# One more five-product step and a rewritten program order in a fused 3x3 convolution with 2x2 max pooling

## The chip, the core and the metric

The kernel runs on one core of one Trainium2 chip. The metric is the device time of one execution in microseconds (us): the median of several runs. The core has five engines that run side by side and meet through semaphores. TensorE (PE) multiplies matrices into the eight banks of PSUM; PEld is its weight load, which overlaps its matmuls. VectorE (DVE) and ScalarE (ACT) work elementwise on SBUF and PSUM. GpSimd (POOL) works on SBUF alone and issues the casting loads of the input. SyncE (SP) issues the other loads and the stores. Each engine takes its instructions strictly in program order.

## The reference

```python
batch, c_in, h, w, c_out, k = 16, 64, 64, 64, 128, 3        # pool_size 2, float32
x_pad = np.pad(x, ((0, 0), (0, 0), (1, 1), (1, 1)))
conv[b, co] += weight[co, ci, kh, kw] * x_pad[b, ci, kh:kh+h, kw:kw+w]   # over ci, kh, kw
output[b, c, i, j] = np.max(conv[b, c, 2*i:2*i+2, 2*j:2*j+2])
```

The input is 16.8 MB, the output 8.4 MB, and every output pixel is the maximum over a 2x2 patch of the convolution.

## The kernel before

**Tiling.** Two images sit on the 128 partitions, 64 input channels each. So there are eight image pairs p, and each pair is cut into four quarters of 16 input rows, which give 8 pooled rows (8x64 elements, 512 on a partition, until the columns are pooled too). A quarter of a pair is a *step* s (0 to 31), and h (0 or 1) is the image within the pair. A *product* is three matmuls, one for each column of the 3x3 kernel, of 64 contraction rows, 128 output channels and 8x64 (or 8x63 at an edge) columns. The products of the two images run on the two halves of the array at the same time; the kernel keeps one lane of products for each half and issues them tap by tap in turn (function `product`, lines 269 to 275), so the k-th product of one lane always goes with the k-th of the other. In this text `P2.7.0|PA1.10.1` is such a couple: name, step, image.

**Two kinds of step.** With g0, g1, g2 the three rows of the kernel and x0, x1 the two input rows of a pooled pair (x before is x-1, x after is x2), the even and odd convolution rows are g0 x-1 + g1 x0 + g2 x1 and g0 x0 + g1 x1 + g2 x2. A *K step* takes **five products**: PA1 and PA2 make (g2-g1) x1 + g0 x-1 in bank ta, PB1 and PB2 make (g0-g1) x0 + g2 x2 in bank tb, and after their maximum PR adds g1 (x0+x1) for both. A *W step* takes **four**: P2 makes half of (g0+g2-g1)(x0-x1) in ta, a copy of it seeds tb, P0 and P3 add products of the row differences x1-x-1 and x2-x0, and after the maximum P1 adds half of (g0+g1+g2)(x0+x1). The string TYPES says which step is which: before, K are 0, 2, 4, 12 and 21 and 27 are W.

**What surrounds the products of one step and image**, in this order:

- row work on SBUF, for both images at once: a K step needs KS (row sum, DVE). A W step needs E (row difference, 512 elements a partition), D (edge differences, 1024) and S (row sum, 512), each on DVE or on POOL by the three lists at lines 40 to 42 (lines 88 and 89)
- SE, W steps alone: ACT copies ta into tb (line 389)
- EV: ACT copies ta out of PSUM, negated in a W step (373, 375)
- MX: DVE takes the row maximum of tb and EV's copy, in place in PSUM (399)
- PR or P1 on PE, and then OD: ACT copies the odd columns out (405)
- CM: DVE takes the column maximum into an output tile (419); ST: SP stores the tile (443)

Each image of a step holds one or two of the eight PSUM banks from its first product until CM. There are 11 output tiles, so the twelfth step to begin its CM waits until the first has been stored.

**The start.** Step 0, 1, 2 and 3 read image pair 0, which SP loads in float32 in pieces: `kfirst` (two pieces, for step 0), `ksecond` (two, for step 2), `middle` (three, for steps 1 and 3; the last piece is issued by the step L). The rows of the two K steps are cast into `kx0` by eight small casts: XOa and XOb (odd rows), XEa and XEb (even rows) of `kfirst`, X1a, X1b, X2a and X2b of `ksecond`. The weights land in `wraw`; g0, g1, g2 and their sums and differences D2, D0, GM, GP are cast into `wq`. For each of them PE transposes its columns (steps TD2, TG0 and so on: a *turn*) and ACT or DVE copies the result to `wt` (VD2, VG0 and so on, lines 180 to 188); TMP and VMP do GM and GP together. POOL repeats a column for three of them (uG1, uGM, uGP) and makes the sum GS. The products of steps 0 and 2 are cut in halves, F.k.part and H.k.part, those of step 1 in G.k.part, and the last P1 in Q.0 and Q.1. The other seven pairs come as 14 loads LX.p.part on POOL's queue, each a half of a pair, cast to bf16 on the way.

**What sets the order.** The schedule is written out: the string ORDER (line 494) lists every step above, and the loop at lines 555 to 557 issues each one's instructions to its engine as it comes. There is no reordering afterwards. A GpSimd operation on SBUF is put behind the last SBUF operation that was given to VectorE ahead of it in ORDER (`on_vector`, `on_gpsimd`, `behind`, lines 74 to 84), also where the data would not ask for it.

Of the kernel before, what the change touches and what calls it, by code (L numbers as in the profile page):

```python
# [11 lines left out]
def kernel(  # L12
# [435 lines left out]

    def cast_rows(n, src, to, lo, hi):
        out, in_ = kx0[:, to + lo : to + hi : 2, :], src[:, lo:hi:2, :]  # L450
        if n in CAST_BY_SCALAR:
            odd_cast[n] = nc.scalar.copy(out=out, in_=in_)
        else:
            odd_cast[n] = nc.vector.tensor_copy(out=out, in_=in_)  # L454

    steps = {
        "g0": lambda: nc.scalar.copy(out=slots(G0), in_=g0),
        "g1": lambda: nc.vector.tensor_copy(out=slots(G1), in_=g1),  # L458
        "g2": lambda: nc.scalar.copy(out=slots(G2), in_=g2),
# [133 lines left out]
```

## Time and profile before

| | |
|---|---|
| median of 3 runs | 102.99 us (102.98 to 103.02) |
| the profiled execution, its own time | 103.01 us |
| its span, first to last instruction | 101.1 us |
| PE busy (94.3 us) | 93% of the span |
| DVE busy (89.9 us) | 89% |
| ACT busy (86.0 us) | 85% |
| POOL busy (70.2 us) | 69% |
| read from HBM, written to it | 17.20 MB, 8.39 MB |

How to read it: a line of the profile names the source line, the engine, the operation, what it writes and reads, and how often it ran; behind the bar stand the busy time of the group, the mean duration of one, and the idle time of the engine just ahead of them with what ended it. Successive instructions of DVE, ACT and PE overlap by some tens of nanoseconds, so a duration is a little more than what an instruction costs its engine; that cost is read from runs of equal instructions in the timeline. The span is 1.9 us shorter than the execution's own time, and what lies around the span is taken as unchanged.

### The profile page before, as it was taken

How to read it: one execution, taken by the hardware profiler on the slowest of the kernel's cores; microseconds unless marked ns; L12 is line 12 of the kernel's file. 1: busy time of each engine (PE TensorE's matmuls, PEld its weight loads, DVE VectorE, ACT ScalarE, POOL GpSimd, SP SyncE). 2: the span in 40 equal slices, each digit the busy share in tenths (PEclk: the TensorE clock that was granted, in tenths of full speed). 3: DMA queues.
4: the chain of work that ended last, by engine and by line, in shares of the span. 5: the costliest groups of instructions: out<-in, count | busy, mean ns of one | idle time of the engine just before them, and what ended most of it. 6: DMA issues, size and time to landing. Idle time of an engine off the chain costs nothing.

```text
span 101.1 us, 2529 instructions
## 1 busy us (share of the span) xinstructions
PE 94.3 (93%) x903; PEld 58.9 (58%) x903; DVE 89.9 (89%) x190; ACT 86.0 (85%) x194; POOL 70.2 (69%) x79
## 2 busy tenths in 40 slices
PE   6889999999999999999999999999999999999900
PEld 2257878844555656777678677675555546545500
DVE  1589989999999999999999989999898969999950
ACT  5356778999699899999999999898999999999830
POOL 7268999906995985774987693994969699417000
PEclk9999999999999999999999999999999999999997
DMA  2999899999947999999947984835024837423062
GB/s 58 297 342 300 171 199 216 221 232 226 244 78 131 247 228 220 228 221 358 343 31 124 282 180 42 169 114 208 3 76 141 304 111 252 163 104 110 0 227 84
DMA packets 11900, 18.41 MB, mean 182 GB/s; under 512 B 880, under 2 KB 9200, under 8 KB 11888
## 3 DMA queue, kind: packets, MB, share of 16 engines
q0 software_dynamic: 2016, 7.34, 39.9%
q1 hardware_dynamic: 9728, 10.78, 32.0%
q8 instruction: 7, 0.11, 0.4%
q10 hardware_dynamic: 144, 0.13, 0.4%
q14 instruction: 5, 0.04, 0.1%
HBM read 17.20 MB, written 8.39 MB: 253 GB/s over the span
## 4 chain that ended last, share of the span: by engine, by line
PE 87%; DVE 4%; DMA 3%; ACT 1%; issue 1%; DVEq 0%; ACTq 0%
PE acc L207 86%; DMA wraw<-in_weight_dram 3%; DVE acc L399 1%; PE acc L165 1%; DVE wq L88 1%; DVE o L434 1%; DVE kx L454 1%; ACT acc L389 1%; ACT od L427 1%; DVE wq L458 0%; DVE wt L188 0%; DVEq L399 0%; ACTq L389 0%
## 5 line engine op out<-in xcount | busy, mean ns | idle before, releaser
L207 PEld LDWEIGHTS <-wt 64*128 64x128 bf16 x870 | 56.4, 94 | 32.6 <-issue 4.7
L207 PE MATMUL acc<-wd,wt 64*128 64x512 bf16 (+2 forms) x336 | 65.9, 369 | 0.1
L399 DVE TENSOR_TENSOR acc<-acc,ev 128x512 f32<-128x512 f32 x64 | 42.4, 692 | 1.4 <-ACT ev L375 0.5
L207 PE MATMUL acc<-we,wt 64*128 64x512 bf16 (+3 forms) x168 | 39.2, 369 | 0.0
L207 PE MATMUL acc<-ws,wt 64*128 64x512 bf16 (+3 forms) x168 | 37.7, 369 | 0.2 <-DVE acc L399 0.2
L375 ACT ACTIVATE ev<-acc 128x512 f32<-128x512 f32 x54 | 32.2, 607 | 1.4 <-PE acc L207 1.2
L389 ACT COPY acc<-acc 128x512 f32<-128x512 f32 x52 | 30.7, 596 | 0.9 <-DVE o L419 0.2
L419 DVE TENSOR_TENSOR o<-acc,od 128x256 f32<-128x256 f32 x62 | 24.4, 417 | 2.4 <-ACT od L405 1.5
L89 POOL TENSOR_TENSOR ws<-xb 128x512 bf16<-128x512 bf16 x15 | 17.1, 1148 | 11.6 <-DVE wd L88 7.3
L405 ACT COPY od<-acc 128x256 f32<-128x256 f32 x62 | 22.5, 382 | 2.1 <-PE acc L207 1.8
L89 POOL TENSOR_TENSOR we<-xb 128x512 bf16<-128x512 bf16 x16 | 18.4, 1150 | 6.0 <-PE acc L207 2.3
L89 POOL TENSOR_TENSOR wd<-xb 128x1024 bf16<-128x1024 bf16 x9 | 19.1, 2123 | 1.9 <-DVE we L88 1.1
L207 PE MATMUL acc<-xb,wt 64*128 64x504 bf16 (+3 forms) x72 | 15.0, 372 | 0.0
L88 DVE TENSOR_TENSOR wd<-xb 128x1024 bf16<-128x1024 bf16 x16 | 10.7, 682 | 0.0
L124 POOL DMA_DIRECT2D xb<-in_x_dram x14 | 7.9, 574 | 0.1
L207 PE MATMUL acc<-ks,wt 64*128 64x504 bf16 (+1 forms) x30 | 7.2, 377 | 0.0
L373 ACT COPY ev<-acc 128x512 f32<-128x512 f32 x10 | 5.6, 590 | 1.4 <-PE acc L207 1.3
L207 PE MATMUL acc<-kx,wt 64*128 64x252 bf16 (+3 forms) x96 | 6.0, 267 | 0.4 <-DVE kx L454 0.4
L89 POOL TENSOR_TENSOR wd<-middle 128x512 bf16<-128x512 f32 (+1 forms) x3 | 4.9, 1643 | 0.2 <-DVE we L88 0.2
L551 PE MATMUL acc<-const-bfloat16-1.0 128*128 128x512 bf16 x8 | 3.5, 621 | 0.8 <-PEq L574 0.8
L88 DVE TENSOR_TENSOR ws<-xb 128x512 bf16<-128x512 bf16 x10 | 4.1, 418 | 0.0
L88 DVE TENSOR_TENSOR we<-xb 128x512 bf16<-128x512 bf16 x9 | 3.7, 425 | 0.0
(33 smaller groups left out, 29.4 us busy)
## 6 DMA issues: line engine op xcount, KB each, us to landing
out_dram<-o SPq DMA_DIRECT2D x31, 256.0 KB, 2.9
xb<-in_x_dram POOLq DMA_DIRECT2D x7, 528.0 KB, 9.0
xb<-in_x_dram POOLq DMA_DIRECT2D x7, 496.0 KB, 11.0
middle<-in_x_dram SPq DMA_DIRECT2D x1, 512.0 KB, 5.3
ksecond<-in_x_dram SPq DMA_DIRECT2D x1, 320.0 KB, 5.8
middle<-in_x_dram SPq DMA_DIRECT2D x1, 320.0 KB, 6.2
wraw<-in_weight_dram SPq DMA_DIRECT2D x1, 288.0 KB, 2.9
kfirst<-in_x_dram SPq DMA_DIRECT2D x1, 288.0 KB, 3.2
```

Of the source, the lines that this page charges most:

```text
L88: return on_vector(nc.vector.tensor_tensor(**args))
L89: return on_gpsimd(nc.gpsimd.tensor_tensor(**args))
L124: inst = nc.gpsimd.dma_start(out=xb[p][:, 1 + lo : 1 + hi, :], in_=rows_of(p, lo, hi))
L165: nc.tensor.transpose(tp[:, k * CO : (k + 1) * CO], wq[:, j : j + 2, :].rearrange("a b c -> a (b c)"), ident,)
L207: nc.tensor.matmul(acc[t][:, i0:i1, o0:o1], wt[lo : lo + CI, tap_of(m0, kw, h), :], rows(lo, i0, i1, c0, c1), start=start and kw == 1, sto ...
L373: nc.scalar.copy(out=ev[s, h], in_=acc[t])
L375: nc.scalar.mul(ev[s, h], acc[t], -1.0)
L389: nc.scalar.copy(out=acc[tb[s, h]], in_=acc[ta[s, h]])
L399: nc.vector.tensor_tensor(out=t, in0=t, in1=ev[s, h], op=MAX)
L405: nc.scalar.copy(out=od[s, h], in_=acc[tb[s, h]][:, :, 1::2])
L419: nc.vector.tensor_tensor(out=ot[s][:, h], in0=acc[t][:, :, 0::2], in1=od[s, h], op=MAX)
L551: nc.tensor.matmul(acc[n].rearrange("p a b -> p (a b)"), ones[:, 0:128], ones, start=True, stop=True, skip_group_check=True)
```

## The change

- TYPES: K steps are 0, 2, 4, 10, 16 and 23, so 26 steps are W instead of 27.
- SUM_ON_GPSIMD, DIFF_ON_GPSIMD, EDGES_ON_VECTOR: the row work is split anew. In numbers, with steps 0 to 3 left out: S on POOL 17 (15 before), on DVE 7 (10); E on POOL 16 (16), on DVE 8 (9); D on DVE 16 (16), on POOL 8 (9); KS on DVE 4 (3).
- Casts and turns: XEa, XOb, XEb and X2a go to ACT (XOb alone before). VG2 goes from ACT to DVE. g0 and g2 stay on ACT, g1 on DVE, though they are now named in the list.
- g1 and the casts that run on DVE are now noted by `on_vector`, so that POOL's SBUF operations further on in ORDER are put behind them.
- ORDER is rewritten as a whole, with the loads LX and the stores ST at other places in it.

```diff
-    TYPES = "KWKWKWWWWWWWKWWWWWWWWKWWWWWWWWWW"
-    SUM_ON_GPSIMD = (5, 7, 8, 9, 10, 14, 15, 18, 19, 20, 23, 24, 28, 29, 30,)
-    DIFF_ON_GPSIMD = (5, 6, 8, 10, 15, 16, 17, 18, 19, 20, 22, 25, 27, 28, 29, 30,)
-    EDGES_ON_VECTOR = (7, 8, 9, 10, 11, 14, 15, 17, 18, 19, 23, 24, 27, 29, 30, 31,)
-    TURNED_BY_SCALAR = ("D2", "G1", "G2", "MP")
-    CAST_BY_SCALAR = ("XOb",)
+    TYPES = "KWKWKWWWWWKWWWWWKWWWWWWKWWWWWWWW"
+    SUM_ON_GPSIMD = (5, 6, 8, 9, 11, 12, 13, 18, 19, 20, 21, 22, 24, 25, 27, 28, 30,)
+    DIFF_ON_GPSIMD = (5, 7, 11, 12, 13, 14, 17, 18, 19, 24, 25, 26, 27, 28, 29, 31,)
+    EDGES_ON_VECTOR = (6, 8, 9, 11, 13, 14, 15, 17, 18, 19, 22, 24, 25, 26, 27, 31,)
+    TURNED_BY_SCALAR = ("D2", "G1", "MP")
+    CAST_BY_SCALAR = ("g0", "g2", "XEa", "XOb", "XEb", "X2a")
...
+    def tap_cast(n, m, src):
+        if n in CAST_BY_SCALAR:
+            nc.scalar.copy(out=slots(m), in_=src)
+        else:
+            on_vector(nc.vector.tensor_copy(out=slots(m), in_=src))
...
-            odd_cast[n] = nc.vector.tensor_copy(out=out, in_=in_)
+            odd_cast[n] = on_vector(nc.vector.tensor_copy(out=out, in_=in_))
...
     ORDER = """
-        D0 g2 g0 TD0 g1 D2 TD2 VD0 XEa uG1 TG1 F.2.0 TG0 XOa L VD2 F.0.0 TG2 GS GP uGP VG1 XOb F.0.1 LX.1.0 VG2
-        VG0 F.1.0 F.1.1 XEb F.2.1 EV.0.1 EV.0.0 GM uGM LX.2.0 F.3.1 F.3.0 TMP VMP KS.0 X1a X2a X1b X2b KS.2
-        H.0.0 H.1.0 H.0.1 H.1.1 EV.2.1 EV.2.0 Ea LX.1.1 LX.3.0 Da MX.0.0 MX.0.1 H.2.0 PR.0.1 H.3.0 G.0.0 Eb
-        G.0.1 H.2.1 H.3.1 PR.0.0 SEa.0 SEa.1 SEb.0 SEb.1 E.3 P2.3.1 G.1.0 S.1 MX.2.0 OD.0.0 CM.0.0 G.2.0 OD.0.1
-        CM.0.1 ST.0 LX.3.1 LX.2.1 Db G.1.1 EV.1.1 MX.2.1 G.2.1 MX.1.1 PR.2.0 PA1.4.0 PA2.4.0 EV.1.0 MX.1.0
...
-        P1.29.1 OD.30.0 CM.30.0 EV.31.1 MX.31.1 EV.31.0 MX.31.0 Q.0 Q.1 OD.30.1 CM.30.1 ST.30 OD.29.0 CM.29.0
-        OD.29.1 CM.29.1 ST.29 ODh.0.0 CMh.0.0 ODh.0.1 CMh.0.1 ODh.1.0 CMh.1.0 ODh.1.1 ST.31.0 CMh.1.1 ST.31.1
+        g0 g2 D0 TD0 D2 TD2 TG0 TG2 XEa g1 uG1 VD2 XOb XEb X2a XOa L VG0 VD0 F.0.0 F.1.0 F.2.0 F.2.1 GS GM TG1
+        F.0.1 F.1.1 LX.1.0 GP VG2 F.3.1 F.3.0 uGM KS.0 X1a H.0.0 H.1.0 LX.1.1 LX.2.0 uGP TMP X1b H.0.1 H.1.1 X2b
+        KS.2 EV.0.0 VG1 Ea Eb EV.0.1 MX.0.1 PR.0.1 MX.0.0 LX.5.1 Da Db D.3 LX.2.1 S.1 H.2.0 VMP G.0.0 G.0.1
+        H.3.0 EV.2.1 H.2.1 H.3.1 MX.2.1 EV.2.0 MX.2.0 SEa.0 SEa.1 SEb.0 SEb.1 PR.0.0 OD.0.0 CM.0.0 OD.0.1 CM.0.1
+        G.2.0 G.1.1 G.1.0 EV.1.1 G.2.1 MX.1.1 PR.2.1 PR.2.0 PA1.4.0 PA2.4.0 E.3 PA1.4.1 PB1.4.0 P2.3.0 PA2.4.1
+        KS.4 EV.1.0 OD.2.0 CM.2.0 MX.1.0 P1.1.0 P2.3.1 P1.1.1 EV.4.1 OD.2.1 CM.2.1 S.5 LX.3.0 LX.4.1 SE.3.1
+        P0.3.1 PB2.4.0 P3.3.1 D.6 E.6 P2.6.1 OD.1.1 CM.1.1 EV.4.0 P2.6.0 OD.1.0 CM.1.0 SE.3.0 P0.3.0 P3.3.0
+        PB1.4.1 MX.4.0 S.3 EV.3.1 MX.3.1 SE.6.1 PR.4.0 P0.6.1 PB2.4.1 EV.3.0 MX.3.0 MX.4.1 SE.6.0 P3.6.1 P0.6.0
+        EV.6.1 MX.6.1 P3.6.0 P1.3.0 P1.3.1 EV.6.0 MX.6.0 OD.4.0 CM.4.0 PR.4.1 OD.3.0 CM.3.0 OD.3.1 CM.3.1 OD.4.1
+        CM.4.1 E.7 E.5 S.6 P1.6.1 P2.5.1 P2.5.0 SE.5.0 P1.6.0 OD.6.0 PA1.10.1 PA2.10.1 P2.7.0 CM.6.0 OD.6.1
...
+        OD.5.1 CM.5.1 P1.5.0 OD.5.0 CM.5.0 OD.7.0 CM.7.0 OD.7.1 CM.7.1 ST.2 ST.1 ST.4 ST.0 ST.3 P0.8.0 EV.8.0
...
+        OD.28.0 CM.28.0 P3.29.1 ST.25 ST.20 ST.26 ST.23 ST.28 SE.30.1 EV.29.1 E.31 D.30 P0.30.0 EV.30.0 P0.30.1
+        P2.31.1 P2.31.0 EV.30.1 P3.29.0 P3.30.1 S.29 D.31 MX.29.1 P1.29.1 P3.30.0 SE.31.0 P0.31.0 P3.31.0
+        SE.31.1 P0.31.1 P3.31.1 S.31 MX.29.0 P1.29.0 S.30 MX.30.0 P1.30.0 MX.30.1 P1.30.1 EV.31.0 MX.31.0
+        EV.31.1 MX.31.1 Q.0 Q.1 OD.29.0 CM.29.0 OD.29.1 CM.29.1 ST.29 OD.30.0 OD.30.1 CM.30.0 CM.30.1 ST.30
+        ODh.0.0 ODh.0.1 ODh.1.0 CMh.0.0 CMh.1.0 ODh.1.1 ST.31.0 CMh.0.1 CMh.1.1 ST.31.1
     """
```

More of the change, by code (lines that the diff above doesn't have):

```diff
@@ L453, in cast_rows @@
         else:
-            odd_cast[n] = nc.vector.tensor_copy(out=out, in_=in_)
+            odd_cast[n] = on_vector(nc.vector.tensor_copy(out=out, in_=in_))
     steps = {
-        "g0": lambda: nc.scalar.copy(out=slots(G0), in_=g0),
-        "g1": lambda: nc.vector.tensor_copy(out=slots(G1), in_=g1),
-        "g2": lambda: nc.scalar.copy(out=slots(G2), in_=g2),
+        "g0": lambda: tap_cast("g0", G0, g0),
+        "g1": lambda: tap_cast("g1", G1, g1),
+        "g2": lambda: tap_cast("g2", G2, g2),
         "D2": lambda: sbuf_sum(True, out=slots(D2), in0=g2, in1=g1, op=SUB),
```

81 lines of the change are left out of this document (36 added, 45 removed).

## The prediction

> **What bounds the kernel now.** I read the page first, then the chain that ended last, then stretches, then timelines of single engines.
>
> ```profile
> PE 94.3 (93%) x903; PEld 58.9 (58%) x903; DVE 89.9 (89%) x190; ACT 86.0 (85%) x194; POOL 70.2 (69%) x79
> PE 87%; DVE 4%; DMA 3%; ACT 1%; issue 1%; DVEq 0%; ACTq 0%
> L399 DVE TENSOR_TENSOR acc<-acc,ev 128x512 f32<-128x512 f32 x64 | 42.4, 692 | 1.4 <-ACT ev L375 0.5
> L389 ACT COPY acc<-acc 128x512 f32<-128x512 f32 x52 | 30.7, 596 | 0.9 <-DVE o L419 0.2
> ```
>
> The chain is 87% PE. Of the others DVE and ACT are close behind, and hardly idle ahead of their largest groups. Whether PE itself runs without gaps is seen from its timeline: two couples of products that follow each other, and the first and last products.
>
> ```profile
> 6.11 0.51 PE L207 MATMUL acc<-kx,wt 64*128 64x256 bf16 x6 [0.44 <-DVE kx L454]
> 6.55 0.40 PE L165 MATMUL acc<-ident,wq 128*128 128x128 bf16 x4
> 6.88 0.50 PE L207 MATMUL acc<-kx,wt 64*128 64x256 bf16 x6
> 7.31 0.40 PE L165 MATMUL acc<-ident,wq 128*128 128x128 bf16 x4
> 7.64 2.06 PE L207 MATMUL acc<-kx,wt 64*128 64x256 bf16 x36
> 9.64 0.51 PE L165 MATMUL acc<-ident,wq 128*128 128x128 bf16 x6
> 10.08 2.14 PE L207 MATMUL acc<-kx,wt 64*128 64x256 bf16 x36
> ...
> 19.30 0.83 PE L207 MATMUL acc<-xb,wt 64*128 64x512 bf16 x6
> 19.95 0.83 PE L207 MATMUL acc<-we,wt 64*128 64x512 bf16 x6
> ...
> 95.41 0.83 PE L207 MATMUL acc<-ws,wt 64*128 64x256 bf16 x12 [0.19 <-DVE acc L399]
> ```
>
> A couple of full products (six matmuls, three on each half) takes 19.95 - 19.30 = 0.65 us; the half products take half of it. By the order there are 121 full couples (one of them short by an edge row: 0.57) and 24 halves (two of them short: 0.24); with 0.648 for a couple these make 85.9 us. The stream of products runs from 6.11 to 95.41 + 0.83 = 96.24, 90.1 us. The three turns inside it take what the next product is late: 6.88 - 6.55 + 0.11 = 0.44, again 0.44 and 0.55, together 1.4. So PE waits only 90.1 - 85.9 - 1.4 = 2.8 us in all. Where?
>
> ```profile
> 6.10:25.00 18.90, 18.79 (x238) 13.06 (x239) 18.08 (x39) 14.89 (x34) 14.60 (x16) 1.00 1.05 235
> 25.00:70.00 45.00, 44.98 (x414) 30.00 (x415) 43.99 (x94) 42.12 (x96) 34.70 (x31) 1.00 0.85 194
> 70.00:81.00 11.00, 11.00 (x105) 6.03 (x102) 9.90 (x21) 10.95 (x27) 9.33 (x7) 1.00 0.37 128
> 81.00:96.30 15.30, 15.00 (x136) 8.02 (x130) 14.10 (x29) 14.31 (x33) 8.23 (x7) 1.00 0.34 119
> ```
>
> The columns after the length are busy time of PE, PEld, DVE, ACT and POOL, the granted clock, DMA share and GB/s. The last stretch has 136 matmuls; 124 full at 0.108 and 12 half ones make 14.0, so it waits about 1.3 of 15.3. Up to 25 us it waits some 0.8; the 56 us between lose only 0.7. The clock is 1.00 throughout. The bound is therefore the PE stream: its start, its work, and waits of a few tenths, where DVE or ACT is a little late.
>
> **The change, part by part.**
>
> *The sixth K step.* One W step's four products become five: one couple more. By the rows above that is +0.65 (the edge rows that are skipped do not change it: in both orders one couple alone is short in both lanes). It takes two SE copies from ACT: 2 x 0.49 = -1.0, and from DVE a net three S and one E less, one KS more. These lie beside PE and count only through waits.
>
> ```profile
> 83.72 1.09 ACT L389 COPY acc<-acc 128x512 f32<-128x512 f32 x2
> 17.97 0.93 ACT L405 COPY od<-acc 128x256 f32<-128x256 f32 x3
> 85.29 1.09 DVE L419 TENSOR_TENSOR o<-acc,od 128x256 f32<-128x256 f32 x3 [0.20 <-ACT od L405]
> 20.89 0.41 DVE L88 TENSOR_TENSOR ks<-xb 128x512 bf16<-128x512 bf16 x1
> 21.22 0.68 DVE L88 TENSOR_TENSOR wd<-xb 128x1024 bf16<-128x1024 bf16 x1
> 21.82 0.41 DVE L88 TENSOR_TENSOR we<-xb 128x512 bf16<-128x512 bf16 x1
> 24.13 2.48 DVE L399 TENSOR_TENSOR acc<-acc,ev 128x512 f32<-128x512 f32 x4
> ```
>
> (From one start to the next: SE 1.09 - 0.596 = 0.49, and EV, of the same shape, I take as that; OD (0.93 - 0.38)/2 = 0.27; on DVE a 512-element row operation 21.22 - 20.89 = 0.33, D 0.60, MX (2.48 - 0.69)/3 = 0.60, CM (1.09 - 0.42)/2 = 0.33.) DVE gets 3 x 0.33 = -1.0 in the long part.
>
> *The start.* Now the first product is F.2.0, and it waits for XEa on DVE.
>
> ```profile
> 3.65 0.50 DVE L88 TENSOR_TENSOR wq<-wraw 128x192 bf16<-128x192 f32 x1 [2.51 <-DMA wraw<-in_weight_dram]
> 4.47 0.49 DVE L88 TENSOR_TENSOR wq<-wraw 128x192 bf16<-128x192 f32 x1
> 5.21 1.04 DVE L454 CAST kx<-kfirst 128x320 bf16<-128x320 f32 x2
> 5.04 0.80 POOL L89 TENSOR_TENSOR gsum<-wraw 128x192 f32<-128x192 f32 x1
> L454 DVE CAST kx<-kfirst 128x320 bf16<-128x320 f32 x1 | 0.8, 848 | 0.0
> L454 DVE CAST kx<-ksecond 128x320 bf16<-128x320 f32 x2 | 0.6, 362 | 0.0
> 4.09 0.53 ACT L457 CAST wq<-wraw 128x192 bf16<-128x192 f32 x1
> 5.45 0.97 ACT L184 COPY wt<-acc 128x512 bf16<-128x512 bf16 x2 [0.83 <-PE acc L165]
> ```
>
> XEa took 848 ns where casts of the same size took 362: it ran while GpSimd's GS did, and lost 0.5. In the changed order the first product is F.0.0, which needs VD2 (ACT) and XOa (DVE). DVE does D0 at 3.65 and D2 at 4.06, so TD2 can run at 4.6 to 5.0 (in the profile D2 came at 4.47, and its turn at 5.0). ACT does g0, g2, XEa, then VD2 from about 5.03, as long as 0.58, to 5.6. DVE is at XOa by 4.9 (0.28). So F.0.0 starts near 5.66: **-0.45**. Behind it VG0 (5.3 to 5.7) and VD0 (to 6.0) are ahead of F.1.0 at 6.0 and F.2.0 at 6.3, and XEb (ACT, 6.6) just ahead of F.2.1.
>
> GS now waits for XOa, a cast on DVE; behind GS stand LX.1.0, uGM, LX.1.1 and LX.2.0 on POOL, and GM and GP on DVE. XOa ends near 5.2, when POOL is still in uG1, so the new wait costs nothing. If a GpSimd copy and XOa do meet, the loss has XEa's 0.5 as its upper bound. I take 0, since VD2 is late to 5.6 anyhow.
>
> The Trainium skill, page "SBUF — State Buffer", section "Who interferes with whom", says that a DVE cast which uses two ports and a GpSimd operation exclude each other, and whichever issues first keeps the pair to its end. XEa's 848 ns agrees. By that rule uG1, which issues about 0.1 us after XOa, would wait for it; were it first, XOa would end near 5.7 and the sum would lose 0.1.
>
> *Turns.* TG0 and TG2 are done ahead of the first product, under the wait for VD2; TG1 (three transposes, 0.4) comes into the stream instead. So two turns of 0.44 go and one of 0.4 comes: **-0.5**.
>
> Together the start and the turns bring the products forward by 0.9 at about 13 us, and the question is what is late next.
>
> *Up to 25 us.* First, DVE. Adding its work in order from the rows above, with the reduce S.1 (1024 elements) as two MX, 1.2, it reaches D.6 near 17.7, MX.4.1 ends near 22.9 and PR.4.1 on PE is ready for it near 22.6: a wait of 0.4. Second, the loads.
>
> ```profile
> 11.41 1.12 POOL L124 DMA_DIRECT2D xb<-in_x_dram  x2
> xb<-in_x_dram POOLq DMA_DIRECT2D x1, 496.0 KB, 14.3
> 12.52 3.61 POOL L89 TENSOR_TENSOR wd<-middle 128x512 bf16<-128x512 f32 x2
> ```
>
> The fifth x load, issued at 11.41, lands 14.3 later, at 25.7; the loads stand in a row and the DMA engines are full (1.05 in the first stretch). The fifth is now LX.2.1, behind LX.5.1. POOL issues it after D.3 (by the third row Db and D.3 take 3.6, Da as long as Db, 1.25, and the three begin behind Eb, near 10.7), near 15.6, still ahead of its turn. The first is released by XOb, which I put at 6.3 on ACT, and 32 KB less stand in front: I take 25.3. PE is at PA1.10.1 with 17.9 us of product work done: 5.66 + 0.9 of turns + 17.9 + 0.4 = 24.9. Wait 0.4. With 0.1 for Db, that is 0.9 where there were 0.8: **+0.1**. Bounds: 0.2, if DVE and load waits overlap, to 1.8, if the load is 25.7 and DVE is held once more by D.6's own load.
>
> *25 to 81 us.* ACT needs 2.5 us for a W step (two each of SE, EV and OD), DVE 1.87 for MX and CM plus its share of row work, PE 2.59. A K step takes PE 3.24 and ACT 1.5, and so gives both others time. Three of them (10, 16, 23) in place of two: I take **-0.2** off the 0.7 us of waits, with bounds -0.6 and +0.8 (the first stretch's waits once more, if DVE is as late there).
>
> *The last 15 us.* Eight W steps follow the last K step instead of ten, so ACT enters the end with less behind it. Against that, ahead of Q both images of steps 29 and 30 still lack OD and CM: four CM in place of three, and S.29 moves to DVE. From CM.28.0 DVE has 7.4 us of work left with PE at 80.8 of 86.6; before, MX.28.1 had 10.4 left with PE at 76.9 of 85.9. Over the whole of PE's work that is 88.1 - 86.6 = 1.5 beyond PE, against 87.3 - 85.9 = 1.4. So I leave the end at **0**, bounds -0.8 and +0.8. PE's end to the span's end (4.8) stays: DVE's queue after the last MX is four CM and four half ones, 4 x 0.33 + 0.21 x 4 = 2.2, and from the last MX's end to the last half CM's it was 97.66 - 95.35 = 2.3:
>
> ```profile
> 94.02 1.33 DVE L399 TENSOR_TENSOR acc<-acc,ev 128x512 f32<-128x512 f32 x2
> 96.55 1.11 DVE L434 TENSOR_TENSOR o<-acc,od 128x128 f32<-128x128 f32 x4 [0.16 <-ACT od L427]
> ```
>
> *Stores and other loads.* The stores of steps 0 to 4 go out together when CM.7 is done, near 32 us. Step 12 reuses the tile of step 0; its CM comes with 38.0 us of products done, near 45.5. So ST.0 has some 13 us.
>
> ```profile
> out_dram<-o SPq DMA_DIRECT2D x2, 256.0 KB, 11.1
> DMA to landing us min/median/max: 1.9/2.6/13.7
> ```
>
> The first row is the two stores at 29.2 to 29.8, beside four x loads: one took 13.7, the longest of all, and so the other 2 x 11.1 - 13.7 = 8.5. That cover is just enough; cost 0, and if it is gone, CM.12 holds all later MX on DVE by what is missing. The other loads (3.1, 4.0, 5.0, 7.0 from about 26 to 30 us) are each used more than 8 us later. KS.23 done early costs DVE the same 0.33.
>
> The Trainium skill, page "DMA: Bandwidth & Descriptors", section "Queues, rings and completion order", says each DMA engine takes turns between its queues packet by packet. By it a store would get turns beside the loads at once and be done in a few us, and CM.12 could not wait; the 13.7 us shows it waiting for the loads, and the measurement decides.
>
> **Sum** against the profiled 103.01: +0.65 - 0.45 - 0.5 + 0.1 - 0.2 + 0 = -0.4, so 102.6. The median of the runs is 0.02 lower. I predict 102.6.
>
> **Rivals.**
>
> 1. *Slower: tiles not stored.* CM.12.1 and CM.11.1 stand on DVE until ST.0 and ST.2 have landed. For it: 13.7 us at the worst, with four loads, and now five stores are beside them. Against: the loads are issued earlier than the stores. It decides from a landing of 45.5 us on; landing 1.5 later gives 102.6 + 1.5 = 104.1.
> 2. *Slower: the fifth load.* LX.2.1 behind LX.5.1 lands at 26.3 or later, for instance because POOL issues it late: everything behind P2.7.0|PA1.10.1 waits, +1.0: 103.6. Against: four loads are ahead of it in any case.
> 3. *The relief is larger.* The waits were there because DVE and ACT were full; with 1.0 less on each, the last 15 us lose 0.5 instead of 1.3 and the middle 0.2: 101.5. For it: ACT busy 10.95 of 11.00 at 70 to 81. Against: DVE's end, as summed.
> 4. *It cancels.* The 0.9 at the start is eaten by loads and DVE before 25 us, the couple more costs 0.65, and relief pays for that: 103.0. For it: DMA share 1.05.
>
> **How the numbers follow.** A difference of 0.2% (0.2 us) is about what a measurement of this kernel can tell from none: faster is below 102.78, slower above 103.2. The forecast's case (102.0 to 102.8, its own range) has 0.40, rival 3 0.17, rival 4 0.20, rival 1 0.11, rival 2 0.12. Faster: 0.17 + 0.40 less 0.02 for its edge at 102.8, 0.55. Same: 0.02 + 0.20 less 0.01 for the edge at 103.2, 0.21. Slower: rivals 1 and 2 and that 0.01, 0.24. Range: the unknown terms add up to about -1.6 and +1.2 (not all at once), so 101.3 to 103.8.
>
> **What would show it.** First product near 5.66, after VD2; one turn of three and one of six transposes inside the stream; PR.0 near 12.6; a PE wait at PR.4.1 and at PA1.10.1, the latter ended by a DMA; CM.12 without a wait for a store; waits of PE after 81 us near 1.3. The prediction is wrong if the first product stays at 6.1, if PE waits more than 1.5 us before 30 us, or if DVE's idle time is ended by a store.

## The result and the profile after

The changed kernel takes 102.00 us in the median of six runs (101.72 to 102.63); the kernel before, run beside it, 102.98. The ratio is 0.991, with a 95% interval of 0.988 to 0.994: 0.9% faster, about 1 us. A second set of six runs gave 102.19 (101.92 to 102.61) and 0.9925 [0.990, 0.995].

Two executions of the changed kernel were profiled: the first took 102.63 us (span 100.8), the second 101.92 (span 100.2). They show the same kernel with two different starts, so both are read here. Line numbers behind the start are 6 higher than before: the warm-up matmuls are line 557, casts of rows line 458 on ACT and 460 on DVE.

First the page of the first one: busy times, the chain that ended last, DVE's largest group and ACT's second largest, the two that were shown of the kernel before.

```profile
PE 94.6 (94%) x909; PEld 56.1 (56%) x909; DVE 88.1 (87%) x185; ACT 84.9 (84%) x194; POOL 69.9 (69%) x80
PE 70%; DVE 10%; POOL 8%; DMA 3%; issue 3%; ACT 2%; DVEq 0%
L399 DVE TENSOR_TENSOR acc<-acc,ev 128x512 f32<-128x512 f32 x64 | 42.7, 692 | 2.8 <-ACT ev L375 1.7
L389 ACT COPY acc<-acc 128x512 f32<-128x512 f32 x50 | 29.5, 599 | 2.3 <-PE acc L207 1.6
```

PE has six matmuls more, DVE and ACT 1.8 and 1.1 us less work. Both now stand idle ahead of these groups for longer: 2.8 us where DVE had 1.4, 2.3 where ACT had 0.9. PE is still the bound.

The start of that execution on PE:

```profile
0.78 3.57 PE L557 MATMUL acc<-const-bfloat16-1.0 128*128 128x512 bf16 x8 [0.78 <-PEq L580]
4.58 1.87 PE L165 MATMUL acc<-ident,wq 128*128 128x128 bf16 x16 [0.23 <-DVE wq L88]
6.38 1.55 PE L207 MATMUL acc<-kx,wt 64*128 64x256 bf16 x24
7.86 0.34 PE L165 MATMUL acc<-ident,wq 128*128 128x128 bf16 x3
8.13 2.14 PE L207 MATMUL acc<-kx,wt 64*128 64x256 bf16 x36
10.21 0.51 PE L165 MATMUL acc<-ident,wq 128*128 128x128 bf16 x6
...
89.56 0.82 PE L207 MATMUL acc<-wd,wt 64*128 64x512 bf16 x6 [0.25 <-POOL wd L89]
```

and of the second one:

```profile
0.78 3.20 PE L557 MATMUL acc<-const-bfloat16-1.0 128*128 128x512 bf16 x8 [0.78 <-PEq L580]
4.33 1.17 PE L165 MATMUL acc<-ident,wq 128*128 128x128 bf16 x16 [0.35 <-DVE wq L88]
5.73 1.45 PE L207 MATMUL acc<-kx,wt 64*128 64x256 bf16 x24 [0.23 <-ACT wt L184]
7.12 0.34 PE L165 MATMUL acc<-ident,wq 128*128 128x128 bf16 x3
7.39 2.14 PE L207 MATMUL acc<-kx,wt 64*128 64x256 bf16 x36
9.47 0.51 PE L165 MATMUL acc<-ident,wq 128*128 128x128 bf16 x6
```

In both, 16 transposes (four turns) stand ahead of the first product, and three and six stand in the stream, where three groups stood before (4, 4 and 6). In the first execution the 16 took 1.87 us, some 107 ns from one start to the next; in the second 1.17, with 55 ns. So the first product came at 6.38 in the one and 5.73 in the other, against 6.11 before. From there on the two run in parallel, 0.65 to 0.75 apart.

Then the stretches of the first one, from its first product on. The columns are those of the prediction's table.

```profile
6.38:25.00 18.62, 18.57 (x237) 11.80 (x238) 17.69 (x37) 13.99 (x34) 15.69 (x17) 1.00 1.05 237
25.00:70.00 45.00, 45.00 (x417) 27.44 (x415) 43.60 (x92) 42.26 (x97) 33.18 (x31) 1.00 0.77 188
70.00:81.00 11.00, 11.00 (x106) 6.21 (x104) 10.18 (x22) 10.33 (x25) 8.18 (x8) 1.00 0.31 108
81.00:96.00 15.00, 14.61 (x138) 7.98 (x134) 13.11 (x27) 14.17 (x33) 9.66 (x7) 1.00 0.44 152
```

From 70 to 81 us ACT is busy 10.33 of 11.00 where it had 10.95. PE's waits are summed from the distances between the starts of its matmuls, each less its columns at 0.427 ns (0.648 us for a couple, as in the prediction). The turns are what is lost at a turn in the stream, its own time included.

| us | before | after, 102.63 | after, 101.92 | predicted change |
|---|---|---|---|---|
| first product | 6.11 | 6.38 | 5.73 | -0.45 |
| product work | 85.91 | 86.48 | 86.49 | +0.65 |
| turns in the stream | 1.41 | 1.00 | 0.96 | -0.5 |
| waits up to 25 us | 0.69 | 0.42 | 0.34 | +0.1 |
| waits 25 to 81 us | 0.46 | 0.56 | 0.62 | -0.2 |
| waits after 81 us | 1.36 | 0.86 | 0.88 | 0 |
| last matmul but one starts | 95.95 | 95.70 | 95.01 | -0.4 |

The last matmul itself starts at 95.97, 95.79 and 95.10. Half of the waits after 81 us is the one in front of 89.56: 0.45 between the starts beyond the matmul's own time, 0.25 of it with PE idle in its row. It ends with D.30 on POOL.

### The profile page after: what moved, and what is told of

Same layout as the page of the kernel before. It is cut to its first block, busy times and chain, and to the rows that moved or that the text cites. A ratio compares the mean times of both kernels' runs of the same rounds, so it can differ in the third digit from the quotient of the medians.

```text
span 100.8 us, 2533 instructions
## 1 busy us (share of the span) xinstructions
PE 94.6 (94%) x909; PEld 56.1 (56%) x909; DVE 88.1 (87%) x185; ACT 84.9 (84%) x194; POOL 69.9 (69%) x80
## 4 chain that ended last, share of the span: by engine, by line
PE 70%; DVE 10%; POOL 8%; DMA 3%; issue 3%; ACT 2%; DVEq 0%
PE acc L207 68%; DVE acc L399 5%; POOL wd L89 4%; DMA wraw<-in_weight_dram 3%; PE acc L165 3%; DVE o L419 2%; POOL ws L89 2%; POOL we L89 1%; DVE wd L88 1%; ACT ev L375 1%; ACT acc L389 1%; DVE wq L88 1%; DVE o L434 0%; ACT od L427 0%; DVE we L88 0%
## 5 line engine op out<-in xcount | busy, mean ns | idle before, releaser
L207 PEld LDWEIGHTS <-wt 64*128 64x128 bf16 x876 | 52.9, 94 | 35.7 <-issue 2.4
L207 PE MATMUL acc<-wd,wt 64*128 64x512 bf16 (+2 forms) x324 | 60.8, 369 | 0.3 <-POOL wd L89 0.3
L207 PE MATMUL acc<-we,wt 64*128 64x512 bf16 (+3 forms) x162 | 37.0, 369 | 0.0
L207 PE MATMUL acc<-ws,wt 64*128 64x512 bf16 (+3 forms) x162 | 36.0, 369 | 0.1
L375 ACT ACTIVATE ev<-acc 128x512 f32<-128x512 f32 x52 | 31.0, 613 | 1.8 <-PE acc L207 1.4
L389 ACT COPY acc<-acc 128x512 f32<-128x512 f32 x50 | 29.5, 599 | 2.3 <-PE acc L207 1.6
L89 POOL TENSOR_TENSOR ws<-xb 128x512 bf16<-128x512 bf16 x17 | 19.4, 1148 | 8.0 <-DVE ws L88 2.7
L207 PE MATMUL acc<-xb,wt 64*128 64x504 bf16 (+3 forms) x96 | 19.4, 372 | 0.0
L89 POOL TENSOR_TENSOR wd<-xb 128x1024 bf16<-128x1024 bf16 x8 | 16.9, 2123 | 0.0
L373 ACT COPY ev<-acc 128x512 f32<-128x512 f32 x12 | 7.0, 593 | 0.8 <-PE acc L207 0.8
```

What stands on the lines that cost most here:

```text
L89: return on_gpsimd(nc.gpsimd.tensor_tensor(**args))
L207: nc.tensor.matmul(acc[t][:, i0:i1, o0:o1], wt[lo : lo + CI, tap_of(m0, kw, h), :], rows(lo, i0, i1, c0, c1), start=start and kw == 1, sto ...
L373: nc.scalar.copy(out=ev[s, h], in_=acc[t])
L375: nc.scalar.mul(ev[s, h], acc[t], -1.0)
L389: nc.scalar.copy(out=acc[tb[s, h]], in_=acc[ta[s, h]])
```

## The experiments

Four questions: why two executions of one kernel differ by 0.7; which part of the change brings the time; what one K step costs by itself; and what the waits at the end are worth. Each run was timed beside the kernel before; the medians of that one were 103.03 to 103.10.

**1. The changed kernel once more.** No edit.

> The changed kernel unchanged, for its spread and a second profiled execution. In the first one (102.63 us) the 16 transposes of the four turns took 107 ns each, against 55 in the kernel before, because PE had stood 0.3 us before them, and the first product came at 6.38 instead of the predicted 5.66. Theory A: that is what parts the executions near 102.6 from those near 101.8; a profiled execution near 101.8 shows transposes at 55 ns and a first product near 5.7. Rival B: the parting comes from loads or stores later on; the first product is near 6.4 in every execution.

102.19 us (101.92 to 102.61), 0.9925 [0.990, 0.995]. Its profile is the second of the two above: the last of the eight warm-up matmuls already runs faster than the first ones (the eight take 3.20 us and not 3.57), the transposes take 55 ns, and all waits behind them keep their size. So what separates the two executions is the start. It has two parts, as DVE's first sums of the weights show, first execution ahead of second:

```profile
3.93 0.91 DVE L88 TENSOR_TENSOR wq<-wraw 128x192 bf16<-128x192 f32 x2 [2.80 <-DMA wraw<-in_weight_dram]
3.69 0.91 DVE L88 TENSOR_TENSOR wq<-wraw 128x192 bf16<-128x192 f32 x2 [2.55 <-DMA wraw<-in_weight_dram]
```

The weights landed 0.25 later in the first, and the turns began 0.25 later for it. The other 0.4 of the 0.65 is the speed at which PE runs its transposes. Why that speed differs is not shown; the reason given above, that PE had stood ahead of the turns, can't be it, since PE stood 0.23 us there in the first execution and 0.35 in the second.

**2. Two more warm-up matmuls.**

```diff
-    for n in range(8):
+    for n in (*range(8), 7, 7):
```

> The changed kernel with ten matmuls ahead of the turns instead of eight, so that PE does not stand before the first turn; the first turn can start at 5.1 at the latest instead of 4.6 (two more of 0.43). Theory A (slow transposes part the executions): transposes at 55 ns in every execution, first product near 6.0, time 101.9 to 102.1 with a spread under 0.4. Rival B: first product later by the 0.5 of the two matmuls, 102.5, with the same spread of 0.9.

102.53 (102.01 to 103.14, 10 runs), 0.9958 [0.993, 0.9985]. Four of the ten took 103.1, the others 102.0 to 102.6; those four have a mean granted clock of 0.986 to 0.987 over the execution, the others 0.992 to 0.999. The profiled one (102.01) had transposes of 55 ns. Neither theory's numbers came: the spread is 1.1 where A had under 0.4, and the median is B's. Two more matmuls are no remedy. Ten of them at 427 ns end 0.85 later than eight, and transposes of 107 ns would come on top, so late starts would explain the four runs at 103.1; but none of the four was profiled. The mean clock is no proof either: the profiled execution of experiment 9's first kernel has 0.985 with transposes of 55 ns.

**3. The casts noted, alone.** One line of the change in the kernel before: the small casts on DVE are told to POOL, so that GS waits for them.

```diff
-            odd_cast[n] = nc.vector.tensor_copy(out=out, in_=in_)
+            odd_cast[n] = on_vector(nc.vector.tensor_copy(out=out, in_=in_))
```

> The kernel before with one edit: casts on VectorE are noted, so that GpSimd's GS is put behind XOa. Theory E: XEa took 848 ns for GS alone; it then takes about 370, the first product starts at 5.65 instead of 6.11, and the time falls by 0.3 to 0.45, to 102.6. Rival: GS and with it GM, GP and uGP come later and TMP, or the loads, hold PE by as much: 103.0.

102.75 (102.51 to 103.16, 12 runs), 0.9966 [0.995, 0.998]. DVE and PE of the profiled execution (102.56):

```profile
5.28 0.54 DVE L454 CAST kx<-kfirst 128x320 bf16<-128x320 f32 x2
6.75 0.51 DVE L88 TENSOR_TENSOR wq<-gsum,wraw 128x192 bf16<-128x192 f32 x1 [0.93 <-POOL gsum L89]
```
```profile
5.68 0.51 PE L207 MATMUL acc<-kx,wt 64*128 64x256 bf16 x6
```

XEa and XOa take 0.54 together where they took 1.04, and the first product comes 0.43 sooner. GM waits 0.93 for GS instead, and the copy VG0 behind it on DVE is late for it, which costs PE a new wait of 0.10 at 7.64. One line is worth a third of the whole change.

**4. The changed start with the old rest.** All of the new start up to MX.0.0 (engines of casts and turns, order, noted casts), then the order of before, with five K steps.

```diff
-    CAST_BY_SCALAR = ("XOb",)
+    CAST_BY_SCALAR = ("g0", "g2", "XEa", "XOb", "XEb", "X2a")
...
-        D0 g2 g0 TD0 g1 D2 TD2 VD0 XEa uG1 TG1 F.2.0 TG0 XOa L VD2 F.0.0 TG2 GS GP uGP VG1 XOb F.0.1 LX.1.0 VG2
+        g0 g2 D0 TD0 D2 TD2 TG0 TG2 XEa g1 uG1 VD2 XOb XEb X2a XOa L VG0 VD0 F.0.0 F.1.0 F.2.0 F.2.1 GS GM TG1
...
+        KS.2 EV.0.0 VG1 Ea Eb EV.0.1 MX.0.1 PR.0.1 MX.0.0 VMP EV.2.1 EV.2.0 LX.3.0 Da H.2.0 H.3.0 G.0.0 G.0.1
```

> The start of the changed kernel (casts, turns, their engines, steps 0 to 2 up to MX.0.0) and behind it the old order, the old split of row work and five K steps. By the prediction's sum the start is worth -0.95 and what is early is lost again up to 25 us by 0.1 to 0.9: 102.1 to 102.9. Theory A: 102.2 where transposes run at 55 ns, 102.8 where they run at 107. Rival C (the gain lies in the rest of the order): 103.0, no gain.

103.05 (102.61 to 104.38, 12 runs), 0.9998 [0.998, 1.001]: no gain. The profiled execution (103.12) has a late start (first product 6.27): its transposes took 107 ns, and the first piece of `kfirst` landed at 5.25, where it was 4.34 in the second execution of the changed kernel. It has 1.09 us of waits up to 25 us instead of 0.69, the new ones of 0.2, 0.13 and 0.09 between 11 and 15 us, where the two orders meet, and some 0.3 more than before behind 25 us. Its two fastest runs, 102.61 and 102.67, are what 0.4 at the start would give; neither was profiled.

**5. The new rest behind the old start**, first with LX.2.0 ahead of LX.1.1, as the old start has them, then with LX.1.1 ahead, as in the changed kernel. From the first to the second:

```diff
-        VG0 F.1.0 F.1.1 XEb F.2.1 EV.0.1 EV.0.0 GM uGM LX.2.0 F.3.1 F.3.0 TMP VMP KS.0 X1a X2a X1b X2b KS.2
-        H.0.0 H.1.0 H.0.1 H.1.1 EV.2.1 EV.2.0 Ea LX.1.1 Eb MX.0.1 PR.0.1 MX.0.0 LX.5.1 Da Db D.3 LX.2.1 S.1
+        VG0 F.1.0 F.1.1 XEb F.2.1 EV.0.1 EV.0.0 GM uGM LX.1.1 F.3.1 F.3.0 TMP VMP KS.0 X1a X2a X1b X2b KS.2
+        H.0.0 H.1.0 H.0.1 H.1.1 EV.2.1 EV.2.0 Ea LX.2.0 Eb MX.0.1 PR.0.1 MX.0.0 LX.5.1 Da Db D.3 LX.2.1 S.1
```

> The old start (up to Ea) and behind it the changed order, with six K steps and the new split of row work. By the prediction's sum the rest is worth +0.65 + 0.1 - 0.2 = +0.55: 103.5. Rival C, from the two profiles (waits of PE behind 25 us 1.5 instead of 2.0, before that 0.35 instead of 0.8): the rest pays for its 0.65 and gives -0.3: 102.7.

104.66 in the median of four runs (104.48 to 104.84), 1.0155 [1.014, 1.017]; the profiled execution took 107.55, with the first piece of `kfirst` landed as late as 6.21, and isn't among the four. In its profile D.6, and everything behind it on DVE, waits for the third load; then PE waits for E.6:

```profile
22.07 0.69 DVE L88 TENSOR_TENSOR wd<-xb 128x1024 bf16<-128x1024 bf16 x1 [2.89 <-DMA xb<-in_x_dram]
```
```profile
23.15 1.77 PE L207 MATMUL acc<-we,wt 64*128 64x512 bf16 x6 [2.42 <-DVE we L88]
```

This is the price of one pair of loads in the wrong order (1.7 us, from the two medians), and of the kind that the prediction's rival 2 was about. It says nothing of the rest itself, so the loads were put right:

> As rest_only, but with the second x load of the changed order (LX.1.1 ahead of LX.2.0), which rest_only lacked: there D.6 and E.6 stood on DVE until LX.1.1 had landed third, at 22.05, and PE waited 2.8. From the profiled executions: from the first product to the end of the span the kernel before takes 95.0 and the changed one 94.4 to 94.5, of which 0.5 are the two turns; with the old start the rest should thus give 95.0 - 0.1. Theory D (start and rest each give little and need each other): 102.8 to 103.0. Rival C (all of the gain lies in the rest): 102.0 to 102.2.

102.99 (102.90 to 103.10, 12 runs), 0.9984 [0.997, 0.9997], near theory D's value. The rest alone pays for its sixth K step and gains 0.1. Its waits are those of the changed kernel (0.34 up to 25 us, 0.59 to 81, 1.04 behind), the first product is at 6.22, the turns at 1.41.

**6. The new rest, the old start and the noted casts**: experiments 3 and 5 together.

> This is the kernel before with the changed kernel's program from Ea on (the two image loads LX.1.1 and LX.2.0 in the order that did not hurt), and with one word of the changed start, the small casts on DVE noted for POOL. The rest alone gave 0.9984 of the kernel before (102.99), the noted casts alone 0.9966 (102.75, first product at 5.68). Theory A (the parts add, since PE is never late for a reason that time cannot move): 0.995, about 102.55 to 102.65, first product 5.7, the later PE waits of the same size as in the changed kernel; what is then left to the changed kernel's 102.0 to 102.2, some 0.45, is the turns, which go from three in the stream to one and a half. Theory B (the start and the rest need each other: with the products 0.4 us earlier, image loads or DVE are late before 25 us): 102.9 to 103.0, with a PE wait ended by a DMA or by DVE between 12 and 25 us.

102.89 (102.54 to 103.63, 12 runs), 0.9985 [0.996, 1.001]. The two gains don't add. In the profiled execution (102.93) the first product is at 5.74, PR.0 0.37 ahead of experiment 5, and then PE loses 0.31 of it again where PA1.10.1 begins, at 26.17. The fifth image load, LX.2.1, has not landed. Its issue in this kernel, and how long it took:

```profile
L124 POOL DMA_DIRECT2D xb<-in_x_dram x1: 581/581/581, 15.6 to 15.6; - x1
  PEld L207: 0.6, 1
DMA to landing us min/median/max: 10.6/10.6/10.6
```

The same in the changed kernel, second execution, where nobody waits for it:

```profile
L124 POOL DMA_DIRECT2D xb<-in_x_dram x1: 576/576/576, 14.7 to 14.7; - x1
DMA to landing us min/median/max: 9.9/9.9/9.9
```

It lands at 26.1 in the one and 24.6 in the other. The loads move as a row, and the row begins earlier in the changed kernel. POOL with the old start:

```profile
7.38 0.24 POOL L149 COPY wq<-wq 128x64 bf16<-128x64 bf16 x1 [0.60 <-DVE wq L88]
7.64 0.70 POOL L124 DMA_DIRECT2D xb<-in_x_dram  x1
```

and in the changed kernel (second execution):

```profile
6.31 0.70 POOL L124 DMA_DIRECT2D xb<-in_x_dram  x1 [0.21 <-ACT kx L458]
```

In the old start uGP stands ahead of LX.1.0 on POOL and waits for GP on DVE; in the new one it stands behind LX.2.0. So theory B holds at one place, but products that come sooner are half of it. The other half is the noted casts themselves, as POOL of experiment 5's second kernel shows, with the same old start and nothing noted:

```profile
7.13 0.71 POOL L124 DMA_DIRECT2D xb<-in_x_dram  x1
```

There the row of loads begins 0.5 sooner, and the fifth lands at 25.65, 0.47 sooner. With casts noted, GS waits for XOa, GP for GS, and uGP and the loads behind it wait for GP. PE was ready for PA1.10.1 at 25.86; with the load at 25.65 it would not have waited. Four of the twelve runs took 102.54 to 102.59, as if the wait were shorter or missing there; they were not profiled. That the new start is the only way to bring both, sooner products and sooner loads, is not shown: the old start with the noted casts and with the loads moved forward was not run.

**7. A sixth K step alone.** Step 27 becomes a K step in the kernel before; its rows and products are renamed in place (S.27 to KS.27, P2 and P0 to PA1 and PA2, P3 to PB2 with PB1 ahead, P1 to PR). As the products of one lane shift against the other's, the row maximum of one image of step 26 is taken ahead of its last product; that changes what it holds, not the work.

> The kernel before with one more five-product step alone: step 27, in the middle of the ten W steps at its end (P2, SE, P0, P3, P1, S become PA1, PB1, PA2, PB2, PR, KS at the same places; E and D fall away). By the sum: PE work +0.65, and the waits behind 81 us (1.3) shrink by what ACT (1.0) and DVE (0.9) are relieved of there: 103.0 + 0.65 - 0.7 = 102.9 if they were late from being full. Rival: the waits hang on single places of the order and stay: 103.6.

104.30 (104.19 to 105.83, 6 runs), 1.014 [1.008, 1.019]. The product work grows by 0.55, and the waits by 0.7: 0.36 between 25 and 81 us and 0.35 behind. The largest, in rows of PE and DVE:

```profile
82.14 0.37 PE L207 MATMUL acc<-wd,wt 64*128 64x512 bf16 x1 [0.50 <-DVE acc L399]
```
```profile
81.06 0.42 DVE L419 TENSOR_TENSOR o<-acc,od 128x256 f32<-128x256 f32 x1 [0.57 <-ACT od L405]
```

Put into an order made for W steps, the K step costs 1.2, twice its work. That is the rival's case, and more than it named. In the changed order the K step costs its work, and the waits shrink.

**8. The start in another order.** In the changed kernel D2 is turned ahead of D0, VD2 stands ahead of XEa on ACT, and LX.2.1 changes places with LX.5.1.

```diff
-        g0 g2 D0 TD0 D2 TD2 TG0 TG2 XEa g1 uG1 VD2 XOb XEb X2a XOa L VG0 VD0 F.0.0 F.1.0 F.2.0 F.2.1 GS GM TG1
+        g0 g2 D2 TD2 D0 TG0 TD0 TG2 VD2 XEa g1 uG1 XOb XEb X2a XOa L VG0 VD0 F.0.0 F.1.0 F.2.0 F.2.1 GS GM TG1
...
```

> The changed kernel with D2 and its turn ahead of D0, VD2 ahead of XEa on ScalarE, and LX.2.1 and LX.5.1 exchanged. Two profiled executions of the changed kernel differ by 0.65 in the first product (5.73 and 6.38) and by as much in every later time, so what the start wins comes through whole. Theory F: VD2 can start at 4.7 to 5.2 instead of 5.1 to 5.6, first product near 5.3 where transposes run at 55 ns (no gain where they run at 107, since all 16 stand ahead of it), time 101.6 to 101.9. Rival: the loads of the first 10 us (middle, ksecond) hold PE then, 102.1.

102.24 (101.73 to 102.56, 6 runs), 0.9903 [0.987, 0.993]; not to be told from the changed kernel. The profiled execution had transposes of 107 ns again and its first product at 6.04, 0.34 sooner than in the first execution of the changed kernel. Most of that is not the order's: the weights landed at 3.63, 0.28 sooner than in that one, which leaves some 0.06 for it.

**9. The wait for D.30.** S.28 moves from POOL to DVE; then S.29 moves from DVE to POOL as well.

```diff
-    SUM_ON_GPSIMD = (5, 6, 8, 9, 11, 12, 13, 18, 19, 20, 21, 22, 24, 25, 27, 28, 30,)
+    SUM_ON_GPSIMD = (5, 6, 8, 9, 11, 12, 13, 18, 19, 20, 21, 22, 24, 25, 27, 30,)
```

> The changed kernel with one row operation, S.28, moved from POOL to DVE, where DVE has 0.3 us idle ahead of the next row maximum. POOL's row of six operations that ends with D.30 then is done 1.1 us sooner. Theory A (the wait of 0.45 us on PE for D.30 near 88 us is time that is won when it goes): 0.4 less, about 101.7. Theory B (DVE sets the end: from its S.29 near 89.4 to 90.1 on it works without a gap to the last row maximum, so PE only waits longer there): no change, 102.0 to 102.2, the wait for D.30 gone and the wait ahead of the last products grown from 0.3 to about 0.7.

> The changed kernel with S.28 moved from POOL to DVE and S.29 moved from DVE to POOL, where POOL is idle for 2.7 us. Theory B (DVE sets the end): DVE's row of work before the last row maximum begins with D.31 and is 0.33 shorter, PE is in time for it since the wait for D.30 is gone: 0.3 less than the changed kernel, about 101.8, waits of PE after 81 us near 0.5. Theory A (PE's wait for D.30 alone): about 101.7 too, but then the kernel with S.28 alone moved is as fast as this one. Rival C: S.29 is late on POOL or DVE's copies from ACT are not there earlier: no change from S.28 alone.

104.48 (104.01 to 104.61), 1.013 [1.010, 1.016], and 104.45 (104.06 to 104.62), 1.013 [1.010, 1.017]. Neither theory saw this. DVE and POOL of the first of the two:

```profile
84.80 0.41 DVE L419 TENSOR_TENSOR o<-acc,od 128x256 f32<-128x256 f32 x1
85.14 0.42 DVE L88 TENSOR_TENSOR ws<-xb 128x512 bf16<-128x512 bf16 x1
```
```profile
81.27 1.15 POOL L89 TENSOR_TENSOR ws<-xb 128x512 bf16<-128x512 bf16 x1
85.63 2.12 POOL L89 TENSOR_TENSOR wd<-xb 128x1024 bf16<-128x1024 bf16 x1 [3.22 <-DVE ws L88]
```

S.28 stands ahead of D.29 in ORDER. On DVE it becomes the operation that POOL's next one is put behind, and as it runs at 85.14, D.29 waits 3.2 us for an operation whose result it doesn't use. PE then waits 1.34 for D.29 and 1.25 for D.30 where it waited 0.45, 2.1 more, and the time is 2.1 longer than in the second execution of the changed kernel (104.01 against 101.92). So a wait for POOL at this place counts in full.

The same with D.29 moved ahead of S.28 in ORDER:

```diff
-        P3.28.0 MX.28.0 SE.29.1 D.29 P0.29.0 EV.29.0 OD.28.1 CM.28.1 P2.30.0 P2.30.1 SE.30.0 P1.28.0 P0.29.1
...
+        P0.28.1 EV.27.1 MX.27.1 OD.26.0 CM.26.0 SE.28.0 ST.21 ST.22 E.29 S.27 D.29 P1.27.0 P2.29.0 P3.28.1 P1.27.1
```

> The kernel with S.28 on DVE and S.29 on POOL once more, with one step moved in ORDER: D.29 ahead of S.28, right behind S.27, so that D.29 on POOL is no longer put behind S.28 on DVE. POOL then runs E.29, S.27, D.29, E.31, D.30 without the 3.2 us of idle time, and D.30 is done near 88.8 where the changed kernel had 89.5 (times of its first profile). Theory A (the waits of the two runs before came from that order alone, and each tenth that PE waits for POOL there is a tenth of the time): the waits of 1.34 and 1.25 and the old 0.45 are gone, 101.5 to 101.8, less by up to 0.3 more if DVE's shorter row of work before the last row maximum counts. Theory B (with D.30 in time the last products wait for DVE or ACT instead): 102.0 to 102.2, the wait ahead of the last products 0.6 to 0.7. Rival C: D.29 waits on POOL for its buffer, and D.30 is as late as it was: 102.1.

102.49 (102.00 to 102.56, 6 runs), 0.9927 [0.990, 0.9955]: the changed kernel's time again, not less. POOL at the end of the profiled execution (102.50):

```profile
82.88 2.12 POOL L89 TENSOR_TENSOR wd<-xb 128x1024 bf16<-128x1024 bf16 x1
86.19 1.16 POOL L89 TENSOR_TENSOR we<-xb 128x512 bf16<-128x512 bf16 x1 [1.19 <-PE acc L207]
87.30 2.13 POOL L89 TENSOR_TENSOR wd<-xb 128x1024 bf16<-128x1024 bf16 x1
89.38 1.17 POOL L89 TENSOR_TENSOR ws<-xb 128x512 bf16<-128x512 bf16 x1
```

D.29 is done 1.2 us before E.31 can start, since E.31's wait is ended by PE: its tile is still read by a product. So D.30 is as late as it was, and PE waits 0.57 for it. It is rival C, with E.31 in D.29's place: the wait is a loop from PE through the tile to E.31 and D.30 (3.2 us of POOL's work) and back to PE, and taking work off POOL doesn't shorten it. A further tile for E was not tried. The wait ahead of the last products is 0.30 in the changed kernel, in both kernels with S.28 moved and in this one.

This execution also began late, though its transposes took 55 ns:

```profile
4.40 1.17 PE L165 MATMUL acc<-ident,wq 128*128 128x128 bf16 x16 [0.30 <-DVE wq L88]
6.28 1.41 PE L207 MATMUL acc<-kx,wt 64*128 64x256 bf16 x24 [0.70 <-DVE wt L188]
```
```profile
5.28 0.29 DVE L460 CAST kx<-kfirst 128x256 bf16<-128x256 f32 x1 [0.20 <-DMA kfirst<-in_x_dram]
```

The first piece of `kfirst` landed at 5.25, where it was 4.34 in the second execution of the changed kernel; XEa and XOa wait for it, and VD2 and VG0, queued behind them on ACT and DVE, are late. So the start's spread has more causes than PE's speed: the landing of the weights, and of `kfirst`.

## Why the prediction was right or wrong

The sign was right, and the time lies in the range, in its lower half: 102.6 predicted, 102.0 to 102.2 measured, some -0.9 instead of -0.4. That the first profiled execution took 102.63 is luck: there the first product came 0.7 later than forecast, the middle cost 0.3 more than forecast, and the waits up to 25 us and after 81 us, 0.4 and 0.5 shorter than forecast, paid for it.

*The first product: right in one execution, wrong in the other.* 5.73 against 5.66, ended by VD2 as summed. What the step left out is that four turns now stand ahead of it. TD2, TG0 and TG2 were taken as hidden under the wait for VD2; at 107 ns a transpose they aren't. That alone makes it 6.04 (experiment 8, whose order is worth 0.06 at most), and 6.38 with the weights landed 0.28 later, so that in the first execution the prediction's own sign of being wrong, a first product that stays at 6.1, was met. Likewise XOa was taken to be free at 4.9, which holds only while `kfirst` has landed. In the old start both were hidden behind XEa's 848 ns, which end at 6.06 in the kernel before: in experiment 5's execution of 107.55 us the transposes ran at 107 ns and were done at 5.94, still ahead of that.

```profile
4.30 1.64 PE L165 MATMUL acc<-ident,wq 128*128 128x128 bf16 x11
```

Without that cover the time follows the start, 101.7 to 102.6. How much the cover steadies the time isn't settled: with the old start, experiment 5's twelve runs spread by 0.2, the kernel before beside them by 0.8 (102.85 to 103.61 in 23 runs), and no run shows why.

*XEa and GS.* The 848 ns were read rightly: experiment 3 takes GS out of the way and the delay goes.

*The turns*: -0.41 to -0.45 against -0.5, right. *The sixth K step*: +0.58 of work against +0.65. One more K step lies at an edge of its image, and 18 matmuls instead of 12 have one row less (441 or 448 columns for 504 or 512); the sum took the short products as many as before. At 0.427 ns a column, with two halves at work, that is some 0.08.

*Up to 25 us: the first failed step*, +0.1 against -0.3. DVE came as summed: D.6 at 17.74 (17.7 predicted), and MX.4.1, third of the five at the end of this stretch, ends near 23.0 (22.9).

```profile
17.74 0.69 DVE L88 TENSOR_TENSOR wd<-xb 128x1024 bf16<-128x1024 bf16 x1
...
21.08 3.15 DVE L399 TENSOR_TENSOR acc<-acc,ev 128x512 f32<-128x512 f32 x5
```
```profile
25.27 0.37 PE L207 MATMUL acc<-xb,wt 64*128 64x512 bf16 x1
```

(Both of the second execution.) It was PE that was put too early. It reaches PA1.10.1 at 25.27, not 24.9: the product work ahead of that is 25.27 - 5.73 - 0.96 - 0.34 = 18.2, not 17.9, and the 0.34 are waits that fall earlier, near 18 and 21 us. So PE gets to PR.4.1 behind MX.4.1, and that wait doesn't come at all. PR.4.1 starts at 23.31, behind MX.4.1's end near 23.0. Nor does the one at PA1.10.1 come: the load landed at 24.6 (25.3 predicted) in this execution and 25.8 in the first, where PE came at 26.0. The margin is 0.2 to 0.7. Experiment 6, where it is gone, shows that such a wait can come: 0.31 lost at PA1.10.1 to that load, where 0.4 was named, though there the load is late too (26.1).

*25 to 81 us*: -0.2 predicted, +0.1 to +0.15 measured. Two waits of 0.30 and 0.14 near 40 us make most of it. The relief that three K steps were to give there didn't come.

*After 81 us: the second failed step*, 0 against -0.5. I compared DVE's queue with PE's at one point and found both kernels alike. But neither DVE's total nor its end sets these waits any more: what is left is 0.45 for POOL's D.30 and 0.30 ahead of Q, and the several waits of 0.1 to 0.4 of the kernel before are gone. Rival 3 named this relief and its sign (DVE and ACT with work taken off them), at 0.8. That the copies saved don't bring it by themselves is seen from experiment 7, where the K step alone makes those waits longer.

*Rivals 1 and 2.* No idle time of DVE is ended by a store, so tiles were not short. The step on the stores was wrong all the same: SP doesn't hold the stores of steps 0 to 4 until CM.7 is done. The eight stores from 18.6 to 47.0 us in the first execution:

```profile
L443 SPq DMA_DIRECT2D out_dram<-o x8: 372/394/602, 18.6 to 47.0; - x8
DMA to landing us min/median/max: 4.2/11.8/16.9
```

ST.0, issued at 26.73, took those 16.9 and landed at 43.6, 1.9 before the 45.5 from which rival 1 would have decided. It was issued 5 us earlier than the prediction had it, and took 3 longer.

*Outside the span.* The execution's own time is longer than its span by 1.85 to 1.89 us on average in four kernels with the old end, and by 1.77 to 1.80 in those with the new end. So some 0.08 of the change lies where the text ahead of the prediction took nothing to change; why is open.

*What stays open.* The parts alone gave -0.1 (rest), 0 (start) and -0.35 (casts noted, a part of the start), the whole -0.9. Experiment 6 shows one link, the loads. For the start alone, the waits at the seam of the two orders, those further on and a late start explain its profiled execution; how much of its lost gain each took over all its runs was not measured. Nor is it shown which part of the new order takes away the waits after 81 us: no experiment left that part of it out alone.

## What to carry to other kernels

When a change takes away the wait that stands first, list what was hidden under it (here four turns at half speed and the landing of the weights and the first rows): those set the time next, and its spread. A step that moves the products forward uses up the time by which loads land early, and an operation that is put behind another engine's also pushes back the loads that stand behind it (0.47 us here); so look at both. A row operation that changes its engine takes its place in the order with it: one S moved by its list alone cost 2.3 us, since POOL's next operation was put behind it. Before work is taken off an engine that PE waits for, see what starts that engine's own chain; where it is PE's release of a tile, taking work off that engine wins nothing there.

## What the runs showed of the hardware

*PE's speed early on.* The warm-up matmuls took 427 ns each and full products' matmuls 216, transposes 107 or 55. In the second execution the higher rate came at about 3.5 us, in the first at about 6.5, with the same program; the granted clock in the rows reads 1.00 there in both. Of the 14 profiled executions ten have it between 3.3 and 4.5 us and four between 5.6 and 6.6. The Trainium skill, page "TensorE: Matmul & The Clock Gate", Part 1, says that PE starts at half rate and is released after a busy window of some 3.4 us that runs freely, so that the moment depends on the window's phase. The moments span some 3.3 us, no more than one such window, which agrees; the page's other figure, a transition that varies by 0.5 us from run to run, is too small here.

*VectorE and GpSimd exclude each other for SBUF rows too.* In the last kernel D.31 on DVE was issued while S.29 ran on POOL (89.38 to 90.55, quoted above):

```profile
89.92 1.17 DVE L88 TENSOR_TENSOR wd<-xb 128x1024 bf16<-128x1024 bf16 x1
```

It took 1.17 instead of 0.68 and ended 0.54 after POOL did. In the two kernels of experiment 9 ahead of it a 512-element S took 0.53 and a D 0.80 in the same way. The Trainium skill, page "SBUF — State Buffer", section "Who interferes with whom", says that a DVE operation with two SBUF inputs and a GpSimd operation that reads SBUF contend, and that the first to issue blocks the other; the three cases, in all of which POOL was first, agree. With DVE first it was POOL that lost: in experiment 9's second kernel S.29 on POOL, issued at 90.98 behind D.31, took 1.60 instead of 1.15. In the first execution of the changed kernel, none of DVE's 36 row operations on line 88 after 12 us runs beside a POOL one for more than 0.15 us: the order keeps the two apart, and a new split of the row work has to keep that.
